# Alternate accumulators from two PSUM pools in the dense stages, and one projection moved into the end of each memory attention

## The chip, the cores and the metric

The kernel runs on one core of one Trainium2 chip. The metric is device microseconds of one execution (us below). The engines are named as the profile names them: PE (matmuls and transposes), DVE and ACT (vector and scalar work, which also read the matmul results), POOL (elementwise work in SBUF only, as this kernel uses it), and SP, whose queue issues most DMAs. Each engine works through its own instructions in the order in which they were written; semaphores make one wait for another.

## The reference, cut to what matters

Two blocks follow one another on 1024 tokens of width 1024, all in float32. The first has two layers. Each layer projects its input, mixes it in a main branch (layer 0: multi-scale causal pooling; layer 1: forgetting attention) and, beside that, in a cross-attention into 256 memory tokens, and ends in a projection, a residual sum and a layer norm. The second block has a gated MLP and an RWKV-7 mixer side by side and then a mixture of 32 experts. For the change only this much must be seen:

```python
def mixer_sublayer(x, mem, w_in, w_mem_kv, w_out, main_fn):
    h = x @ w_in                       # columns [main | mem q | main gate | mem gate]
    u_main = h[..., :D_MAIN]
    q_mem = h[..., D_MAIN:D_MIX]
    g_main = h[..., D_MIX:D_MIX + D_MAIN]
    g_mem = h[..., D_MIX + D_MAIN:]
    y_main = main_fn(u_main)
    y_mem = memory_attention(q_mem, mem, w_mem_kv)
    y = jnp.concatenate([y_main * jax.nn.silu(g_main), y_mem * jax.nn.silu(g_mem)], axis=-1)
    return y @ w_out
...
# layer 0: main_fn = causal_multiscale_pool(u): trailing means over 2, 4, 8, 16 tokens, one linear map per group
# layer 1: main_fn = forgetting_attention(q, k, v, cum); k, v and the forget gates f from x @ w_kv_shared
# block 2: z = h @ w_in2; gMLP on zu, zv; RWKV-7 on zr (decay, inverse of a triangular matrix per chunk, scan)
```

## The kernel before

**Precision and matmuls.** Every operand of a large product is cut into a high and a low part (`split`, L167; for weights `split_one`, L117): ACT casts the high part (`wh`, `xh`), DVE or POOL subtracts it to get the low part (`wl`, `xl`). One product is three matmuls (`mm3`, L161; lines L163 to L165). A *half* of a dense projection (`proj`, L239) is 8 x 3 = 24 matmuls of 512 columns into one PSUM accumulator; `evac` then reads that accumulator on ACT and DVE.

**PSUM.** Two pools of tiles hold the accumulators: `ps1` with two tiles of one bank (`bank`, L173; they appear in the trace as `mm`), and `ps2` with three tiles of two banks (`banks2`, L179; `at`). A pool hands out its tiles in turn. A tile that is handed out again makes the first matmul into it wait until all that read it before are done. Dense stages take `bank()` only; attention logits, transposes and a few sums take `banks2()`.

**Order.** The program is a list of items, executed in order while it is recorded. `weave` (L182) puts *side* functions among *dense* items: after dense item d stand the side functions whose place is at most d (at most `per` of them), and what is left over follows at the end. Weights are loaded and split two uses ahead.

**Memory attention** (`mem_attention`, L325) has 16 dense halves (q and gate of four heads) and eight units (head, half of the tokens). A unit goes through three steps, each one side function later than the last: `logits` (PE into an `at` tile, then DVE maximum, ACT exponentials, DVE scaling into `P`), `turn` (eight transposes of `P` into an `at` tile, ACT and DVE split them into `PTh`, `PTl`) and `values` (six matmuls, then `y_out`). The last unit's `turn` and the last two `values` follow when the dense halves have run out. In layer 1 the first two halves (`self.first`) stand earlier, and the memory's keys and values come back from DRAM by one DMA (`kvt<-kvd`, L735) at `begin_kv`; the first `logits` stands behind the first half that follows.

**Pooling stage of layer 0** (`u_evac` L629, `mix` L667): for each group of 256 channels two projections u (whose evacuation is a chain of shifted sums on DVE, longer for the wider windows), two gates g, then `mix`, two accumulators for each half of the tokens. `mix(g, 0)` stands ahead of the first half of the next group's u, and `mix(g, 1)` behind it. Each accumulator of `mix` is read by `y_out` (L417): one DVE product into `y32`, a tile with a single buffer (L418), which ACT and POOL then split into `yh` and `yl`.

**Layer 1's projections** (`layer1_proj`): the forget gates f (one projection of 16 columns, `w_f`), q and k (16 projections), v (four groups of eight accumulators of 256 columns, split into `vst`, three buffers, each stored to DRAM), gates. Side functions among them form the 48 partial sums of another product on DVE from DMA'd weights (`ad`), and `mod_sum` closes every fourth with a matmul into an `at` tile (L860).

**gMLP projections** (`gmlp_proj`) of block 2 run while DVE still inverts the RWKV triangles step by step (`rwkv_inverse`, L1466 and L1467); its result goes to DRAM (`Tmd`, `Tnd`) and comes back as `N` and `T` for `rwkv_merge` (L1584), which stands among the gMLP's dense items.

Of the kernel before, what the change touches and what calls it, by code (L numbers as in the profile page):

```python
# [45 lines left out]
class Prog:  # L46


    def __init__(self, tc, ins, out):
        self.tc = tc  # L50
        self.nc = tc.nc
        self.i = ins
        self.out = out
        self.items = []
        self.later = []
        self.lst = {}
        self.lag = 2
        self.item = 0
        self.open = {}


# [110 lines left out]

    def bank(self):  # L173
        return self.ps1.tile([128, 512], F32, name="mm", tag="mm")

# [63 lines left out]
    def proj(self, spec, evac, M=128):  # L239
# [13 lines left out]

        return [(first, [spec]), (lambda: half(1), [])]


# [325 lines left out]
    def layer0(self):  # L582
# [22 lines left out]

        self.add(begin_mem)
        d, s = self.mem_attention(0)
        self.weave(d, s)

        def begin_r():  # L610
# [10 lines left out]
            for t in range(16):  # L621
                nc.vector.memset(self.cnt[:, t:t + 1], 1.0 / (t + 1))

        self.add(begin_r)
        ymem = lambda: self.ymem
        U, PM, SG = {}, {}, {}
        self.ymain = {}
# [55 lines left out]
        def ug(g):  # L683
            it = []
            for j in range(2):
                it += self.proj((self.i["w_in"][0, 2 * g + j], 1024, "g"), u_evac(g, j))
            for j in range(2):
# [13 lines left out]

        def end_pool():
            self.close("pg")
            self.lnp = self.pool("ln", right=True)
# [17 lines left out]
    def layer1_proj(self):  # L722
# [11 lines left out]
        def begin_kv():  # L734
            nc.sync.dma_start(self.open_kv(True).bitcast(F32), self.kvd)  # L735
            self.mp = self.pool("mp", right=True)

        self.add(begin_kv)
        self.weave(self.rest, [(k - 2, f) for k, f in self.side])

        def begin():
            self.close("mp", "kv", "mq")
            self.st = self.pool("st", right=True)

        self.add(begin)
# [65 lines left out]

        dense = self.proj((self.i["w_f"], KD * 16, "g"), f_evac, M=16)
        for p in range(8):
# [66 lines left out]
        self.weave(dense, side, 2)  # L880
        self.add(lambda: self.close("st", "xt"))

# [600 lines left out]
    def gmlp_proj(self):  # L1483
        nc = self.nc

        def begin():
            self.close("rw")
            self.gp = self.pool("gp", right=True)
            self.gate1 = self.row(self.gp, self.modd[:, 2 * D:3 * D], "gate")
            gm = self.gm = self.pool("gm", right=True)  # L1490
            self.gv = gm.tile([128, NT, 512], F32, name="gv")
# [116 lines left out]
    def rwkv_chain(self):  # L1608
# [6 lines left out]

        def begin():
            self.close("ps2")
            self.ps2 = self.pool("ps2", 2, PSUM)
# [1152 lines left out]
```

## Time and profile before

| what | value |
|---|---|
| runs shown (3) | 2796.18, 2798.14, 2799.12 us; median 2798.14 |
| profiled execution | 2806.17 us, of which the span of the core's instructions is 2804.4 us |
| busy in the profiled span | PE 2618.7 us (93%), DVE 1759.6 (63%), ACT 1212.4 (43%), POOL 826.8 (29%) |
| mean granted clock of TensorE | 0.966 of 2.4 GHz |
| layer 0, memory attention | from about 60 us to 183 us of the span |
| layer 0, pooling and output | 183 us to 560 us |
| layer 1, memory attention | 565 us to 681 us |
| layer 1, projections | 681 us to 1065 us |
| block 2, gMLP projections | 1729 us to about 1800 us |

The profiled execution took 8.0 us more than the median of the three timed runs. Times of stretches below count from the start of the span. Idle time of PE costs time only where PE is what the rest waits for; a granted clock of 0.5 means that matmuls come half as fast (1.2 GHz in place of 2.4).

### The profile page before, as it was taken

To read this page: it belongs to the slowest core of one execution; us is meant where nothing else is said; L and a number is where in the kernel's file an instruction comes from. 1 tells how busy PE (TensorE), PEld (TensorE's weight loads), DVE (VectorE), ACT (ScalarE), POOL (GpSimd) and SP (SyncE) were. 2 spreads that over 40 slices of the span, in tenths; PEclk is the share of its full clock that TensorE was granted. 3 is DMA by queue.
4 is the path that set the end of the run, shared out by engine and by line. 5 is a ranking of instruction groups with operands and counts; after the bars stand their busy time and mean duration, and the time that the engine had idled before them with its cause. 6 is when DMAs were issued, how large, how long until landed. Compare 5 with 4: busy or idle time off the path is not lost. (4 is left out here: it accounts for less than half of the span.)

```text
span 2804.4 us, 40099 instructions
## 1 busy us (share of the span) xinstructions
PE 2618.7 (93%) x14955; PEld 2131.7 (76%) x14955; DVE 1759.6 (63%) x2560; ACT 1212.4 (43%) x1851; POOL 826.8 (29%) x480
## 2 busy tenths in 40 slices
PE   8999999999999997999986989999995999999996
PEld 7878787776878886888865667987784777777774
DVE  5332334633556314777867769633657998899998
ACT  5331212333212213667643522323433767677773
POOL 1122323612222121112145432323362332233324
PEclk9999999999999998999998999999996999999999
DMA  7121111311787537655522465466327999899995
GB/s 267 33 91 49 42 48 43 112 55 38 257 299 263 192 104 219 167 156 168 137 79 73 134 188 180 97 156 151 99 95 263 355 349 344 303 376 368 368 367 206
DMA packets 284886, 511.43 MB, mean 182 GB/s; under 512 B 122651, under 2 KB 166027, under 8 KB 284432
## 3 DMA queue, kind: packets, MB, share of 16 engines
q1 hardware_dynamic: 275040, 491.26, 53.5%
q0 software_dynamic: 9360, 16.52, 1.6%
q8 instruction: 119, 1.95, 0.3%
q10 hardware_dynamic: 288, 1.05, 0.1%
q14 instruction: 79, 0.65, 0.1%
HBM read 437.53 MB, written 97.18 MB: 191 GB/s over the span
## 5 line engine op out<-in xcount | busy, mean ns | idle before, releaser
L128 POOL TENSOR_TENSOR wl<-raw,wh 128x1024 fp32r<-128x1024 f32 (+2 forms) x111 | 281.1, 2541 | 663.4 <-ACT wh L126 653.7
L171 DVE TENSOR_TENSOR wl<-raw,wh 128x1024 fp32r<-128x1024 f32 x384 | 452.0, 1223 | 37.8 <-ACT wh L169 37.7
L163 PE MATMUL mm<-xh,wh 128*128 128x512 f32 (+3 forms) x1136 | 452.6, 398 | 12.9 <-DVE y L419 8.5
L165 PE MATMUL mm<-xh,wl 128*128 128x512 f32 (+3 forms) x1136 | 450.4, 397 | 0.7 <-POOL wl L128 0.7
L164 PE MATMUL mm<-xl,wh 128*128 128x512 f32 (+3 forms) x1136 | 450.1, 396 | 0.8 <-DVE xl L171 0.8
L169 ACT CAST wh<-raw 128x1024 fp32r<-128x1024 f32 x384 | 382.7, 1049 | 54.3 <-PE mm L165 21.4
L163 PEld LDWEIGHTS mm<-xh,wh 128*128 128x128 f32 (+3 forms) x1136 | 213.4, 188 | 73.7 <-issue 11.5
L164 PEld LDWEIGHTS mm<-xl,wh 128*128 128x128 f32 (+3 forms) x1136 | 213.4, 188 | 53.2 <-issue 2.0
L165 PEld LDWEIGHTS mm<-xh,wl 128*128 128x128 f32 (+3 forms) x1136 | 213.4, 188 | 50.3 <-POOL wl L128 1.1
L163 PE MATMUL mm<-wh,xth 128*128 128x512 f32 x496 | 202.1, 408 | 2.1 <-ACT xth L169 1.1
L164 PE MATMUL mm<-wl,xth 128*128 128x512 f32 x496 | 200.2, 404 | 3.2 <-DVE wl L171 2.9
L165 PE MATMUL mm<-wh,xtl 128*128 128x512 f32 x496 | 196.7, 397 | 0.0
L126 ACT CAST wh<-raw 128x1024 fp32r<-128x1024 f32 (+1 forms) x139 | 140.0, 1023 | 75.8 <-PE mm L165 74.4
L2408 POOL DMA_INDIRECT ymd<-yo,si x32 | 53.0, 1657 | 381.0 <-DVE yo L2451 377.3
L163 PE MATMUL mm<-wh,yh 128*128 128x512 f32 x384 | 160.2, 417 | 1.5 <-DVE y L419 1.1
L410 DVE SCALAR_TENSOR_TENSOR sg<-sg,mm 128x512 f32<-128x512 f32 x48 | 33.0, 688 | 196.0 <-ACT sg L409 196.0
L163 PE MATMUL mm<-wh,xh 128*128 128x256 f32 x512 | 147.0, 287 | 9.0 <-DVE vst L171 4.0
L164 PE MATMUL mm<-wl,yh 128*128 128x512 f32 x384 | 153.5, 400 | 1.7 <-POOL wl L128 1.7
L165 PE MATMUL mm<-wh,yl 128*128 128x512 f32 x384 | 152.9, 398 | 0.0
L164 PE MATMUL mm<-wl,xh 128*128 128x256 f32 x512 | 143.5, 280 | 0.0
L165 PE MATMUL mm<-wh,xl 128*128 128x256 f32 x512 | 143.4, 280 | 0.0
L2403 POOL DMA_INDIRECT xg<-h2d,gi x33 | 117.2, 3550 | 57.7 <-PE at L2414 27.9
(546 smaller groups left out, 5777.3 us busy)
## 6 DMA issues: line engine op xcount, KB each, us to landing
raw<-in_w_moe_dram SPq DMA_DIRECT2D x382, 512.0 KB
raw<-in_w_in_dram SPq DMA_DIRECT2D x48, 512.0 KB
ad<-in_ada_w_dram SPq DMA_DIRECT2D x48, 512.0 KB
raw<-in_w_out_dram SPq DMA_DIRECT2D x32, 512.0 KB
ymd<-zd SPq DMA_DIRECT2D x16, 512.0 KB
vd<-vst SPq DMA_DIRECT2D x32, 256.0 KB
qa<-qd SPq DMA_DIRECT2D x32, 256.0 KB
kb<-kd SPq DMA_DIRECT2D x32, 256.0 KB
```

Of the source, the lines that this page charges most:

```text
L126: self.nc.scalar.copy(h[:p], r[:p])
L128: e.tensor_tensor(l[:p], r[:p], h[:p].bitcast(F32), ALU.subtract)
L163: mm(ps, ah, bh, start=start, stop=False)
L164: mm(ps, ah, bl, start=False, stop=False)
L165: mm(ps, al, bh, start=False, stop=stop)
L169: self.nc.scalar.copy(h, src)
L171: e.tensor_tensor(l, src, h.bitcast(F32), ALU.subtract)
L410: nc.vector.scalar_tensor_tensor(sg, sg, 1.0, ps, op0=ALU.add, op1=ALU.mult)
L2403: self.nc.gpsimd.indirect_dma_start(out=xg, out_offset=None, in_=self.h2d[:, :], in_offset=bass.IndirectOffsetOnAxis(ap=gi, axis=0), bound ...
L2408: self.nc.gpsimd.indirect_dma_start(out=self.ymd[:, :], out_offset=bass.IndirectOffsetOnAxis(ap=si, axis=0), in_=y, in_offset=None, bounds ...
```

## The change

Three things change. A flag `wide` makes `bank()` hand out tiles of the two pools in turn: one time the first half of a two-bank `at` tile, the next time an `mm` tile. The flag is on in the pooling stage of layer 0 (from `begin_r` to `end_pool`), in layer 1's projections (from `begin` to `end`) and from the start of the gMLP projections to the start of the RWKV chain. Second, `proj_held` is a projection whose two halves write the two halves of one `at` tile, and whose evacuation is a list of items of its own; with it the next stage's first projection (layer 0: the first u; layer 1: f) is appended to the dense halves of the memory attention, and its evacuation stands where the projection stood. Third, in layer 1's memory attention no side function stands ahead of the second dense half.

```diff
@@ def bank(self)
+        if self.wide:
+            self.turnabout = not self.turnabout
+            if self.turnabout:
+                return self.banks2()[:, 0:512]
         return self.ps1.tile([128, 512], F32, name="mm", tag="mm")
...
+    def proj_held(self, spec, evac, M=128):
+        hold = {}
+        def half(h):
+            wh, wl = hold["w"]
+            ps = hold["ps"][:M, h * 512:h * 512 + 512]
+            for k in range(KD):
+                self.mm3(ps, wh[:, k], wl[:, k], self.xh[h][:, k], self.xl[h][:, k], k == 0, k == KD - 1)
+        def first(w):
+            hold["w"] = [t.rearrange("p (k n) -> p k n", k=KD) for t in w]
+            hold["ps"] = self.banks2()
+            half(0)
+        out = [(lambda h=h: evac(h, hold["ps"][:M, h * 512:h * 512 + 512]), []) for h in range(2)]
+        return [(first, [spec]), (lambda: half(1), [])], out
...
@@ def layer0(self)
         d, s = self.mem_attention(0)
-        self.weave(d, s)
+        held, u00 = self.proj_held((self.i["w_in"][0, 0], 1024, "g"), u0)
+        self.weave(d + held, s)
...
+            self.wide = True
...
-                it += self.proj((self.i["w_in"][0, 2 * g + j], 1024, "g"), u_evac(g, j))
+                it += u00 if g + j == 0 else self.proj((self.i["w_in"][0, 2 * g + j], 1024, "g"), u_evac(g, j))
...
         def end_pool():
+            self.wide = False
...
@@ def layer1_proj(self)
+        held, fs = self.proj_held((self.i["w_f"], KD * 16, "g"), lambda h, ps: f_evac(h, ps), M=16)
         self.add(begin_kv)
-        self.weave(self.rest, [(k - 2, f) for k, f in self.side])
+        self.weave(self.rest + held, [(max(k - 2, 1), f) for k, f in self.side])
...
+            self.wide = True
...
-        dense = self.proj((self.i["w_f"], KD * 16, "g"), f_evac, M=16)
+        dense = list(fs)
...
+        def end():
+            self.wide = False
+            self.close("st", "xt")
```

**Place 1, PE at the end of layer 0's memory attention.** Of each block of matmuls the first row stands here: before, the third-last unit's `values` (`mm_1481`), then the last `turn` (`at_1492`), the last two `values`, and the two halves of the first u (`mm_1580`, `mm_1620`) and of the second.

```order
L163 MATMUL mm_1481<-PTh_1363,kvt_119 128x512
...
L367 MATMUL at_1492<-ident_75,P_1458 128x128 x8
L163 MATMUL mm_1505<-PTh_1477,kvt_119 128x512
...
L163 MATMUL mm_1518<-PTh_1501,kvt_119 128x512
...
L163 MATMUL mm_1580<-xh0_112,wh_1264 128x512
...
L163 MATMUL mm_1620<-xh1_113,wh_1264 128x512
...
L163 MATMUL mm_1662<-xh0_112,wh_1380 128x512
```

The same place in the changed kernel:

```order
L164 MATMUL mm_1481<-PTh_1363,kvt_119 128x512
...
L164 MATMUL at_1498<-xh0_112,wh_1264 128x512
...
L391 MATMUL at_1523<-ident_75,P_1458 128x128 x8
L164 MATMUL mm_1536<-PTh_1477,kvt_119 128x512
...
L164 MATMUL at_1498<-xh1_113,wh_1264 128x512
...
L164 MATMUL mm_1573<-PTh_1532,kvt_119 128x512
...
L164 MATMUL at_1661<-xh0_112,wh_1380 128x512
```

The two halves of the first u (24 matmuls each) now stand one ahead of the last `turn` and one ahead of the last `values`, both in the tile `at_1498`; the second u begins in another `at` tile. At the end of layer 1's memory attention the halves of f stand in the same two places.

**Place 2, DVE in the pooling stage,** around the first u half of the group with window 16, between `mix(2, 0)` and `mix(2, 1)`; `y` is the product of `y_out`, `sw` and `pm` are the chain of sums. Before:

```order
L419 SCALAR_TENSOR_TENSOR y_3082<-mm,psc,sg 128x512
L636 MEMSET u 128x16
L642 COPY carry<-u 128x16
L648 TENSOR_TENSOR sw<-u 128x527
L648 TENSOR_TENSOR sw<-sw 128x525
L648 TENSOR_TENSOR sw<-sw 128x521
L648 TENSOR_TENSOR sw<-sw 128x513
L651 SCALAR_TENSOR_TENSOR pm<-sw,u 128x512
...
L654 TENSOR_TENSOR pm<-sw,u 128x15
L419 SCALAR_TENSOR_TENSOR y_3145<-mm,psc,sg 128x512
L419 SCALAR_TENSOR_TENSOR y_3156<-mm,psc,sg 128x512
```

In the changed kernel:

```order
L443 SCALAR_TENSOR_TENSOR y_3081<-mm,psc,sg 128x512
L666 MEMSET u 128x16
L672 COPY carry<-u 128x16
L678 TENSOR_TENSOR sw<-u 128x527
L678 TENSOR_TENSOR sw<-sw 128x525
L678 TENSOR_TENSOR sw<-sw 128x521
L678 TENSOR_TENSOR sw<-sw 128x513
L681 SCALAR_TENSOR_TENSOR pm<-sw,u 128x512
...
L684 TENSOR_TENSOR pm<-sw,u 128x15
L443 SCALAR_TENSOR_TENSOR y_3144<-mm,psc,sg 128x512
L443 SCALAR_TENSOR_TENSOR y_3155<-at,psc,sg 128x512
```

No DVE instruction moves; the second accumulator of `mix(2, 1)` now lies in an `at` tile.

**Place 3, PE at the start of layer 1's memory attention.** First rows of the blocks before: the first half after `begin_kv`, the first `logits` (`at_4025`), the next half, the second `logits`, the first `turn`.

```order
L163 MATMUL mm_3996<-xh1_3479,wh_3831 128x512
...
L163 MATMUL at_4025<-kvt_3991,qh_3925 128x256
...
L163 MATMUL mm_4051<-xh1_3479,wh_3835 128x512
...
L163 MATMUL at_4079<-kvt_3991,qh_4021 128x256
...
L367 MATMUL at_4105<-ident_75,P_4041 128x128 x8
```

In the changed kernel:

```order
L164 MATMUL mm_3995<-xh1_3478,wh_3830 128x512
...
L164 MATMUL mm_4024<-xh1_3478,wh_3834 128x512
...
L164 MATMUL at_4052<-kvt_3990,qh_3924 128x256
...
L164 MATMUL mm_4084<-xh0_3477,wh_3893 128x512
...
L164 MATMUL at_4113<-kvt_3990,qh_4020 128x256
```

The first `logits`, the first reader of the DMA'd `kvt`, stands one dense half later.

## Rows read from the trace of the kernel before

**Rows 1.** The page: busy time, share of the span and count of PE, and PE's clock.

```profile
PE 2618.7 (93%) x14955; PEld 2131.7 (76%) x14955; DVE 1759.6 (63%) x2560; ACT 1212.4 (43%) x1851; POOL 826.8 (29%) x480
PEclk9999999999999998999998999999996999999999
```

**Rows 2.** Timeline of PE, one middle unit: start, duration, instruction, [idle before, releaser].

```profile
94.57 0.28 PE L163 MATMUL at<-kvt,qh 128*128 128x256 f32 x1
...
96.01 1.04 PE L367 MATMUL at<-ident,P 128*128 128x128 f32 x8
96.81 0.48 PE L163 MATMUL mm<-PTh,kvt 128*128 128x512 f32 x1
...
98.28 0.39 PE L163 MATMUL mm<-xh,wh 128*128 128x512 f32 x1
```

**Rows 3.** Timeline of PE, end of layer 0's memory attention.

```profile
167.97 0.28 PE L163 MATMUL at<-kvt,qh 128*128 128x256 f32 x1
...
173.80 1.46 PE L367 MATMUL at<-ident,P 128*128 128x128 f32 x8 [1.97 <-DVE P L359]
...
182.73 0.63 PE L163 MATMUL mm<-xh,wh 128*128 128x512 f32 x1
```

**Rows 4.** Timeline of PE, end of layer 1's memory attention.

```profile
666.25 0.28 PE L163 MATMUL at<-kvt,qh 128*128 128x256 f32 x1
...
680.97 0.63 PE L163 MATMUL mm<-xh,wh 128*16 128x512 f32 x1
```

**Rows 5.** Windows: length, busy of PE PEld DVE ACT POOL, PE's clock, DMA share, GB/s.

```profile
182.73:186.02 3.29, 3.29 (x9) 2.61 (x8) 0.69 (x1) 1.56 (x2) 1.81 (x3) 0.50 0.62 167
338.98:346.00 7.02, 7.02 (x24) 5.60 (x25) 0.83 (x2) 1.22 (x2) 3.81 (x3) 0.76 0.00 0
439.92:448.00 8.08, 8.08 (x24) 6.47 (x25) 0.83 (x2) 1.21 (x2) 3.79 (x3) 0.66 0.00 0
570.41:577.00 6.59, 6.59 (x25) 5.85 (x26) 1.49 (x3) 1.94 (x8) 0.00 (x0) 0.64 0.00 0
1732.00:1750.00 18.00, 13.10 (x90) 12.70 (x89) 17.70 (x16) 5.75 (x8) 7.16 (x2) 0.81 0.59 183
1789.10:1797.00 7.90, 7.90 (x159) 7.69 (x160) 6.87 (x11) 2.54 (x5) 5.96 (x5) 0.78 0.67 179
1073.66:1084.00 10.34, 7.93 (x24) 6.30 (x25) 3.56 (x11) 3.53 (x9) 0.00 (x0) 0.51 1.07 360
1720.00:1771.00 51.00, 45.48 (x330) 42.83 (x330) 50.36 (x39) 14.52 (x23) 21.29 (x7) 0.93 0.40 127
```

**Rows 6.** Timeline of PE, three waits in the pooling stage.

```profile
285.78 0.51 PE L163 MATMUL mm<-xh,wh 128*128 128x512 f32 x1 [1.59 <-DVE y L419]
...
338.98 0.51 PE L163 MATMUL mm<-xh,wh 128*128 128x512 f32 x1 [3.11 <-DVE y L419]
...
439.92 0.79 PE L163 MATMUL mm<-xh,wh 128*128 128x512 f32 x1 [3.85 <-DVE y L419]
```

**Rows 7.** Timeline of DVE, ahead of the third of these waits.

```profile
433.95 1.29 DVE L642 COPY carry<-u 128x16 f32<-128x16 f32 x1 [3.12 <-ACT u L639]
...
439.12 0.74 DVE L419 SCALAR_TENSOR_TENSOR y<-mm,psc,sg 128x512 f32<-128x512 f32 x1
```

**Rows 8.** Timeline of DVE, end of the pooling stage.

```profile
492.12 0.75 DVE L419 SCALAR_TENSOR_TENSOR y<-mm,psc,sg 128x512 f32<-128x512 f32 x1 [2.05 <-POOL yl L171]
```

**Rows 9.** Timeline of PE, start of layer 1's memory attention.

```profile
570.41 0.55 PE L163 MATMUL at<-kvt,qh 128*128 128x256 f32 x1 [4.70 <-DMA kvt<-kvd]
```

**Rows 10.** Waits of PE and of ACT, 720 to 1062 us: total, times, longest.

```profile
PE mm L163 <- DVE vst L171: 4.0, 6, 1.6
...
ACT vst L169 <- DMA vd<-vst: 49.8, 17, 5.7
```

**Rows 11.** Timeline of PE: the wait for `N`, and the first matmul of layer 1's attention.

```profile
1789.10 1.07 PE L1584 MATMUL mm<-N,L 32*32 32x32 f32 x57 [2.00 <-DMA N<-Tnd]
...
1073.66 0.45 PE L940 MATMUL at<-kb,qa 128*128 128x128 f32 x1 [9.12 <-DMA kb<-kd]
```

More of the change, by code (lines that the diff above doesn't have):

```diff
@@ L59, in __init__ @@
         self.open = {}
+        self.wide = self.turnabout = False
     def pool(self, name, bufs=1, space=None, right=False):
@@ L606, in layer0, with u0 @@
         self.add(begin_mem)
+        U, PM, SG = {}, {}, {}
+        def u0(h, ps):
+            u_evac(0, 0)(h, ps)
         d, s = self.mem_attention(0)
-        self.weave(d, s)
+        held, u00 = self.proj_held((self.i["w_in"][0, 0], 1024, "g"), u0)
+        self.weave(d + held, s)
         def begin_r():
@@ L622, in begin_r @@
                 nc.vector.memset(self.cnt[:, t:t + 1], 1.0 / (t + 1))
+            self.wide = True
         self.add(begin_r)
         ymem = lambda: self.ymem
-        U, PM, SG = {}, {}, {}
         self.ymain = {}
@@ L880, in layer1_proj @@
         self.weave(dense, side, 2)
-        self.add(lambda: self.close("st", "xt"))
+        def end():
+            self.wide = False
+            self.close("st", "xt")
+        self.add(end)
     def layer1_fox(self):
@@ L1489, in begin @@
             self.gate1 = self.row(self.gp, self.modd[:, 2 * D:3 * D], "gate")
+            self.wide = True
             gm = self.gm = self.pool("gm", right=True)
@@ L1616, in begin @@
         def begin():
+            self.wide = False
             self.close("ps2")
```

## The prediction, written before the changed kernel was run

> **What bounds the kernel now.** The page comes first: PE is busy for 93% of the span and no other engine for more than 76%, and its clock stands at full speed in most of the 40 slices [rows 1]. So time is to be had only where PE stands still or runs at half clock, and the change can touch three such kinds of place. I read the list of PE's waits, then the timeline of PE around each wait in the stages that the change touches, and last the windows, which give the clock behind each wait. The reader is to see four things. At the end of each memory attention PE has nothing left but a chain of short steps that wait for the softmax [rows 3, 4]. In the pooling stage PE waits three times for `y`, the read of an accumulator, and the row shows a plain projection (`mm<-xh,wh`) waiting: its operands are there, the bank is not [rows 6]. At the start of layer 1's attention PE waits for a DMA [rows 9]. And behind each of these waits the granted clock is at 0.5 for some microseconds [rows 5], so that a wait costs more than its own length. A clock c over a window of w us costs w x (1 - c).
>
> **The change, part by part.** No matmul, evacuation or DMA is added or removed; the sum consists of waits that go or come.
>
> A. *End of layer 0's attention.* From the last `logits` to the first matmul of the next stage the trace takes 182.73 - 167.97 = 14.76 us [rows 3]. The work in it is one `logits`, two `turn` and three `values`. A middle unit shows what these take without waits: 96.01 - 94.57 = 1.44, 96.81 - 96.01 = 0.80, 98.28 - 96.81 = 1.47 [rows 2]; together 1.44 + 1.60 + 4.41 = 7.45. So 7.3 us are lost there, and the next 3.29 us run at 0.50, which loses 1.65 [rows 5]: 8.95 in all. In the changed order a half of 24 matmuls stands between the last `logits` and the last `turn`, and one ahead of the last `values`. Per half that is 24 x 0.229 = 5.5 us (a `values` has six such matmuls in 1.47 to 0.23 each). The wait for `P` to be covered is 1.97 [rows 3]. Both halves cover with margin, so I take all 8.95. What these halves covered before also counts: behind the attention they ran while pools closed and loads landed. Now the second u does that. It has a free `at` tile and a free `mm` tile for its first two halves, some 11 us; only the third half needs an `at` tile that could still be held. I cost this at nothing.
>
> B. *Pooling stage.* The waits of 1.59, 3.11 and 3.85 [rows 6] come from two accumulators in turn: `y` of `mix(g, 1)` stands on DVE behind the whole chain of sums of the u half just evacuated (433.95 to 439.12 in the widest group [rows 7]), and PE's next half needs that `y`'s bank. With tiles taken from both pools in turn, the next half gets a tile whose reader was done a half earlier, so the wait goes, and DVE has until the next `mix`, some six halves on, to catch up. Behind the second and third wait the clock costs 7.02 x 0.24 = 1.7 and 8.08 x 0.34 = 2.7 [rows 5]. Sum: 8.55 + 4.4 = 12.95, which I take as 13.0. Two further waits for `y` stand at the end of the stage, and these I do not count: there four `y` follow one another through the single `y32` buffer, the last at 492.12 [rows 8], `wide` is off for the output items behind it, and the second of those needs just the bank that the last `y` reads. With or without the earlier waits PE gets past it at about 492.9.
>
> C. *Start of layer 1's attention.* The wait for `kvt` is 4.70 [rows 9] and the clock behind it costs 6.59 x 0.36 = 2.4 [rows 5]: 7.1. The half put ahead takes 5.5 > 4.70, so the wait goes, with 0.8 us to spare. Bounds: 6.1 (the DMA a little later) to 7.1.
>
> D. *End of layer 1's attention.* The same pattern: 680.97 - 666.25 = 14.72 [rows 4], less 7.45 is 7.3, and a stretch at half clock as long as A's: 9.0.
>
> E. *v projections.* PE waits for the read of `vst` in six places, 4.0 us [rows 10]. Behind them stands ACT, which waits for the store of an earlier `vst` (49.8 us in 17 waits). More accumulators let PE run two quanta further ahead, which hides a late store but doesn't make stores faster. Bounds 0 and 4.0; I take 3.0, since the longest single wait (1.6) is shorter than one quantum of 24 x 0.12 = 2.9 us (0.12 is a `logits` matmul of the same 256 columns: 1.44 / 12 [rows 2]).
>
> F. *gMLP projections.* Here too two accumulators run short: PE is idle for 18.00 - 13.10 = 4.9 us and the clock is at 0.81 [rows 5], together some 7 to 8 us. But DVE is busy for 50.36 of 51.00 us in this stretch [rows 5]; it works through the inverse, and PE meets the inverse's result soon after, where it already waits 2.0 us for `N` [rows 11]. If PE comes 7.7 us earlier, it waits 9.7 there. Worse, one long wait in place of several short ones can cost more clock: now 7.90 x 0.22 = 1.7 [rows 5]; behind the wait of 9.12 [rows 11] it is 10.34 x 0.49 = 5.1 [rows 5]. Bounds: -3.4 (all of that difference) to +8 (if `N` came as much earlier as PE does). DVE's share speaks for the low end; the loads behind the inverse may go out a little earlier, as POOL frees earlier. I take -2.0.
>
> Sum: 8.95 + 13.0 + 7.1 + 9.0 + 3.0 - 2.0 = 39.05. The profiled execution took 2806.17, so it would take 2767.1; it lies 8.0 above the median, and I subtract from the median: 2798.14 - 39.05 = **2759.1**.
>
> **The rivals.**
> *More accumulators only move the wait* (B and E give nothing, as F). For it: DVE, ACT and the stores work no faster, and in the pooling stage a chain of sums takes about as long as a half. Against: DVE is free for most of that stage, as the gates behind u have no chain of sums, so the backlog has time to drain. Left are A + C + D + F = 23.05: 2775.1.
> [...]
>
> *The cover is missed elsewhere.* The held tile is one of three; it comes free only when its evacuation is done, and that stands behind the closing of pools, a constant's DMA and a bias DMA. If PE's third half has to wait for it, A and D each give back about what they gained: 2759.1 + 18 = 2777. Against: 11 us of other halves stand in between.
>
> *F gains after all:* `N` follows PE. At the upper bound the sum is 10 larger: 2749. Against: DVE's 50.36 of 51.00.
>
> *Slower than before:* in layer 1's projections `mod_sum` now draws its `at` tile from the same ring as the projections, and PE stands behind DVE's partial sums there. There are 12 of them; to eat 39 us each must wait 3.3 us. Before, the list of PE's waits in that stretch has no line but the one for `vst`, 4.0 in all [rows 10], so none of the 12 waited as it was. Some wait here is possible, 3.3 each is not likely: 2800.
>
> *The change does nothing:* the rows of the changed order show the tiles alternating and the halves moved, so only a loss that happens to equal the gain leaves the time where it was.
>
> **How the numbers follow.** Chances: forecast 0.66; accumulators only move the wait 0.12; cover missed 0.08; F gains 0.09; slower 0.03; no change 0.02. The likeliest gives 2759. Its own spread, from the bounds of C, E and F's low end and about 5 us for B, is 2752 to 2768. To leave out no more than 2 in 10 the range takes in the two rivals of 2775 and 2777 and nearly all of 2749: 2748 to 2778. A difference of 0.2% (5.6 us) is about what a measurement of this kernel can tell from none. All cases but the last two are faster by more than that: faster 0.95, same 0.02, slower 0.03.
>
> **What would show each step right or wrong.** A and D: no wait for `P` or `PTh` at either end of attention, the first matmul of the held projection directly behind the third-last `values`, and full clock there. B: no wait of a projection for `y`, but the two at the end of the stage still there, with the last `y` of the stage as far behind its first `mix` as before. C: no wait for `kvt`, or one below 1 us. E: the waits for `vst` below 1 us in all. F: no wait for `gv` or `z` at the gMLP's start, and a wait for `N` of about 10 us with a longer stretch at half clock behind it. What would make the prediction wrong: PE waiting for u's or f's evacuation some 11 us behind the attention, waits at L860's matmuls, or a wait for `N` as short as before.

## The result, and the profile after

| | changed kernel | kernel before |
|---|---|---|
| median | 2763.19 us (2760.01 to 2763.59, 4 runs) | 2798.63 us (2796.18 to 2800.24, 4 runs) |
| ratio | 0.9856, 95% interval 0.9838 to 0.9874 | |
| span, mean granted clock in the profile | 2758.2 us, 0.977 | 2804.4 us, 0.966 |

The medians are 35.4 us apart, where 39 were forecast. The ratio and its interval are the ones on record; they are not the quotient of the two medians (0.9873), and a ratio of 0.9856 would be 40 us. So the total is known to some 5 us, and the terms have to be read from the traces. The page of the changed kernel, PE's busy time and clock (compare [rows 1]):

```profile
PE 2594.9 (94%) x14955; PEld 2118.6 (77%) x14955; DVE 1772.4 (64%) x2560; ACT 1210.8 (44%) x1851; POOL 819.8 (30%) x480
PEclk9999999999999999999998999999997999999999
```

The windows of the changed kernel that answer to [rows 5]: the end of layer 0's attention, the pooling stage without its end, the start and the end of layer 1's attention, layer 1's projections, the gMLP up to `N`, and the wait for `N`:

```profile
165.00:180.00 15.00, 15.00 (x81) 12.81 (x80) 5.13 (x10) 5.43 (x13) 4.00 (x3) 1.00 0.12 36
...
190.00:450.00 260.00, 260.00 (x1128) 211.19 (x1127) 103.85 (x175) 56.70 (x83) 86.41 (x50) 1.00 0.16 51
...
540.00:565.00 25.00, 25.00 (x136) 21.45 (x135) 11.97 (x20) 8.07 (x22) 2.43 (x1) 1.00 0.26 97
640.00:660.00 20.00, 20.00 (x92) 12.08 (x91) 5.56 (x10) 7.99 (x15) 7.92 (x5) 1.00 0.09 28
680.00:1018.00 338.00, 338.00 (x1827) 282.35 (x1826) 154.14 (x189) 66.30 (x105) 75.18 (x30) 1.00 0.66 227
1684.00:1736.00 52.00, 52.00 (x435) 51.66 (x434) 49.92 (x48) 15.12 (x26) 19.35 (x9) 1.00 0.51 128
1736.00:1746.00 10.00, 3.63 (x75) 3.29 (x74) 8.47 (x16) 0.94 (x2) 4.58 (x4) 0.77 0.64 134
```

In the first six PE is busy for all of the time and the clock is at 2.4 GHz throughout; the seventh is what is left. The timeline of PE at the end of layer 0's attention, against [rows 3]: the last `logits`, the held first half of u, the last `turn`, the held second half, and the second u. No row has a wait.

```profile
167.88 0.28 PE L164 MATMUL at<-kvt,qh 128*128 128x256 f32 x1
...
171.57 0.39 PE L164 MATMUL at<-xh,wh 128*128 128x512 f32 x1
...
177.06 1.03 PE L391 MATMUL at<-ident,P 128*128 128x128 f32 x8
...
179.32 0.39 PE L164 MATMUL at<-xh,wh 128*128 128x512 f32 x1
...
186.19 0.39 PE L164 MATMUL at<-xh,wh 128*128 128x512 f32 x1
```

Of the waits in the stages read here, those at the end of the pooling stage stay (the second is the `y` of [rows 8]), and those for `N` and for `kb` [rows 11]. Timeline of PE of the changed kernel:

```profile
464.02 0.50 PE L164 MATMUL mm<-wh,yh 128*128 128x512 f32 x1 [0.66 <-DVE y L443]
...
469.61 0.50 PE L164 MATMUL mm<-wh,yh 128*128 128x512 f32 x1 [2.53 <-DVE y L443]
...
1029.53 0.44 PE L977 MATMUL at<-kb,qa 128*128 128x128 f32 x1 [9.15 <-DMA kb<-kd]
...
1741.83 0.28 PE L1622 MATMUL at<-N,L 32*32 32x32 f32 x2 [4.95 <-DMA N<-Tnd]
1743.53 0.69 PE L1622 MATMUL at<-N,L 32*32 32x32 f32 x18 [1.42 <-DMA N<-Tnd]
```

**Where the time came from.** The same matmul can be looked up in two traces. Its start in the first trace of before less its start in another one is that kernel's *lead* there; at the first `kb` matmul it is 1073.66 - 1029.53 = 44.13. Between two points the lead grows by what the stage gained. Below is the middle value of nine matmuls in a row, for the kernels of the experiments too (us; the left column is the time in before's first trace).

| at | after | before, 2nd trace | after, 2nd trace | wide only | held only | held, early psc | one half | mix alone |
|---|---|---|---|---|---|---|---|---|
| 160, l0 attention | 0.1 | 0.0 | -0.2 | -0.2 | 0.3 | 0.0 | 0.2 | 0.2 |
| 200, behind it | 9.1 | 2.0 | 8.8 | 1.1 | 9.2 | 9.0 | 5.2 | 9.1 |
| 260 | 9.1 | 2.0 | 8.8 | 0.6 | 0.7 | 9.0 | 5.2 | 9.1 |
| 460 | 23.3 | 2.6 | 23.0 | 14.9 | 1.8 | 10.8 | 19.5 | 20.6 |
| 510, behind pooling | 23.3 | 2.6 | 23.0 | 14.9 | 1.8 | 10.9 | 19.5 | 14.3 |
| 590, in l1 attention | 30.2 | 5.1 | 28.3 | 15.9 | 8.7 | 16.2 | 26.4 | 21.2 |
| 700, behind it | 39.0 | 5.9 | 37.1 | 16.8 | 17.5 | 24.3 | 32.9 | 29.3 |
| 1060, behind l1 proj. | 44.2 | 5.9 | 37.1 | 18.7 | 17.1 | 25.9 | 33.5 | 31.0 |
| 1725, ahead of gMLP | 43.5 | 2.3 | 33.8 | 16.0 | 15.3 | 23.5 | 28.7 | 30.1 |
| 1830, behind `N` | 45.1 | -0.2 | 34.1 | 16.8 | 16.7 | 25.2 | 29.3 | 30.6 |
| 2700 | 46.2 | -0.7 | 34.4 | 17.0 | 18.8 | 27.9 | 31.9 | 30.8 |

The terms of the prediction against two pairs of traces, each the step of the lead between the two lines that enclose the stage (for the second pair, the third column less the second):

| term | forecast | first pair | second pair |
|---|---|---|---|
| A, end of l0 attention | 8.95 | 9.0 | 7.0 |
| B, pooling stage | 13.0 | 14.2 | 13.6 |
| C, wait for `kvt` | 7.1 | 6.9 | 2.8 |
| D, end of l1 attention | 9.0 | 8.8 | 8.0 |
| E, v projections | 3.0 | 5.2 | 0.0 |
| F, gMLP | -2.0 | 1.6 | 2.8 |
| stages the change does not touch | 0 | 0.4 | 1.0 |
| sum | 39.05 | 46.1 | 35.2 |

One trace gives a stage no better than to some microseconds: from 1060 to 1725 us, where no kernel here differs from before, the steps of the lead run from -4.8 to 0.5 us over the thirteen traces.

### The profile page after: what moved, and what is told of

It reads as the page before. It is cut to its first block, busy times and chain, and to the rows that moved or that the text cites. A ratio compares the mean times of both kernels' runs of the same rounds, so it can differ in the third digit from the quotient of the medians.

```text
span 2758.2 us, 40093 instructions
## 1 busy us (share of the span) xinstructions
PE 2594.9 (94%) x14955; PEld 2118.6 (77%) x14955; DVE 1772.4 (64%) x2560; ACT 1210.8 (44%) x1851; POOL 819.8 (30%) x480
## 5 line engine op out<-in xcount | busy, mean ns | idle before, releaser
L164 PE MATMUL mm<-xh,wh 128*128 128x512 f32 (+2 forms) x792 | 316.2, 399 | 3.7 <-DVE ca L1301 2.6
L165 PE MATMUL mm<-xl,wh 128*128 128x512 f32 (+2 forms) x792 | 312.6, 395 | 0.8 <-DVE xl L172 0.8
L166 PE MATMUL mm<-xh,wl 128*128 128x512 f32 (+2 forms) x792 | 312.2, 394 | 0.7 <-POOL wl L129 0.7
L164 PEld LDWEIGHTS mm<-xh,wh 128*128 128x128 f32 (+2 forms) x792 | 148.7, 188 | 44.4 <-issue 5.4
L165 PEld LDWEIGHTS mm<-xl,wh 128*128 128x128 f32 (+2 forms) x792 | 148.7, 188 | 35.9 <-issue 1.8
L166 PEld LDWEIGHTS mm<-xh,wl 128*128 128x128 f32 (+2 forms) x792 | 148.4, 187 | 35.5 <-POOL wl L129 1.1
L166 PE MATMUL at<-xh,wl 128*128 128x512 f32 (+1 forms) x344 | 135.3, 393 | 0.0
L164 PE MATMUL at<-xh,wh 128*128 128x512 f32 (+1 forms) x344 | 135.2, 393 | 0.0
L165 PE MATMUL at<-xl,wh 128*128 128x512 f32 (+1 forms) x344 | 134.9, 392 | 0.0
L2442 POOL DMA_INDIRECT xg<-h2d,gi x33 | 114.9, 3481 | 57.7 <-PE at L2453 27.9
L999 ACT ACTIVATE pp<-pp,fst 128x128 f32<-128x128 f32 (+7 forms) x128 | 99.9, 781 | 63.1 <-DVE fst L992 61.7
```

What stands on the lines that cost most here:

```text
L164: mm(ps, ah, bh, start=start, stop=False)
L165: mm(ps, ah, bl, start=False, stop=False)
L166: mm(ps, al, bh, start=False, stop=stop)
L999: nc.scalar.activation(p[:, :n], p[:, :n], AF.Exp, bias=st[:, i:i + 1], scale=-1.0, accum_out=st[:, 8 + i:9 + i])
L2442: self.nc.gpsimd.indirect_dma_start(out=xg, out_offset=None, in_=self.h2d[:, :], in_offset=bass.IndirectOffsetOnAxis(ap=gi, axis=0), bound ...
```

## The experiments

Times are medians; with each stands the ratio on record to runs of the kernel before on the same chip (its median there was 2802.21, 2805.01 and 2801.89 us for the first four, the next four and the last four kernels).

**1. The kernel before once more.** No edit.

> The kernel before once more, for a second profile of it. The first profiled execution took 2806.2 us, 8 us above the median of its timed runs, and the changed kernel's first profile gains 46 us on it where the timed medians differ by 35. Theory: the 8 us are chance of that one execution (which half-clock stretches fall where), so this profile comes out near 2798 and the difference lies in stages that the change does not touch. Rival: a profiled execution of this kernel is always some 8 us longer, then it comes out near 2806 again.

Measured: 2806.41 us (10 runs, 2794.77 to 2812.01), ratio 1.0006 [0.9992, 1.0021]; the profiled execution took 2808.89, its span 2807.2. Neither theory is held up as it was put: this execution was long as well, yet timed runs of the same program spread from 2794 to 2812. What the second trace does show is that the stages are not as long each time. Windows around the end of layer 0's attention and behind the wait for `kvt`, and that wait in PE's timeline:

```profile
165.00:190.00 25.00, 20.98 (x94) 16.33 (x93) 8.71 (x33) 7.84 (x16) 7.09 (x5) 0.93 0.61 207
567.00:574.00 7.00, 6.54 (x34) 5.68 (x35) 2.57 (x7) 1.94 (x8) 0.00 (x0) 1.00 0.00 0
...
567.46 0.36 PE L163 MATMUL at<-kvt,qh 128*128 128x256 f32 x1 [2.71 <-DMA kvt<-kvd]
```

The same first window in the first trace of before:

```profile
165.00:190.00 25.00, 21.27 (x86) 16.10 (x84) 7.65 (x13) 7.28 (x16) 7.10 (x5) 0.80 0.56 195
```

In the attention's end the waits are nearly the same (for `P` 4.0 us in two, one at each attention, as in the first trace) and the clock is higher, 0.93 against 0.80; so A loses 2 us less in this execution than in the one that the sum was made from. The wait for `kvt` is 2.71 in place of 4.70, and no half clock follows it, where [rows 5] has 0.64. But here a stretch at half clock lies ahead of the wait (0.51 over 558.90 to 562.30; the first trace has full clock in that half), so that by the lead C loses 2.5 us less, and not the 4 that the wait and the clock behind it would give.

**2. Only the alternating accumulators.** The two held projections and the later first `logits` are taken back:

```diff
...
-        self.weave(d + held, s)
+        self.weave(d, s)
...
-                it += u00 if g + j == 0 else self.proj((self.i["w_in"][0, 2 * g + j], 1024, "g"), u_evac(g, j))
+                it += self.proj((self.i["w_in"][0, 2 * g + j], 1024, "g"), u_evac(g, j))
...
-        self.weave(self.rest + held, [(max(k - 2, 1), f) for k, f in self.side])
+        self.weave(self.rest, [(k - 2, f) for k, f in self.side])
...
-        dense = list(fs)
+        dense = self.proj((self.i["w_f"], KD * 16, "g"), f_evac, M=16)
```

> Only the alternating accumulators, no held projection, layer 1's side functions where they were. Theory (the stages' gains are local and add up): the two ends of attention and the DMA wait stand as before, 9 + 7 + 9 = 25 us are lost again, the pooling stage gains 14, the v projections 6 and the gMLP 1.5: 2798.6 - 21.5, about 2777. Rival (accumulators only move waits): near 2798, with new waits of PE later in the same stages.

Measured: 2787.84 us, ratio 0.9945 [0.9927, 0.9963]: between the theory's 2777 and the rival's 2798. PE's waits from 160 to 700 us (total, times, longest) have those of the two attentions again, and of `y` only the end of the stage:

```profile
PE at L164 <- DMA kvt<-kvd: 4.4, 1, 4.4
PE at L391 <- DVE P L383: 3.9, 2, 2.0
PE mm L164 <- DVE y L443: 3.2, 2, 2.5
PE mm L164 <- ACT PTh L170: 2.3, 2, 1.2
```

The lead grows by 14.3 from 260 to 460 us, so the pooling stage's gain needs no held projection. What the theory had too high is the rest: in the gMLP the lead grows by 0.8 (1725 to 1830), not by 1.5, and in the v projections by 1.9 (700 to 1060), not by 6: the waits for `vst` are gone, and in their place stands another (total, times, longest; 700 to 1040 us):

```profile
PE at L891 <- DVE acc L883: 3.4, 4, 1.2
```

That is `mod_sum`, the place of the slower rival, but what is late is not its accumulator: it is the partial sum `acc` itself. PE comes there sooner, and DVE itself waits there for the DMA of its weights `ad` (2.3 us in four).

**3. Only the held projections.** `self.wide = True` is taken out in all three places.

> Only the held projections and the later first logits; bank() hands out mm tiles alone everywhere. Theory: A 9.0 + C 6.9 + D 8.8 = 24.7 us of the gain stay: about 2774. Rival (the held halves only pay because the wide stage behind them absorbs the late evacuation): PE waits for u's or f's accumulator behind the attention, and the time is above 2780.

Measured: 2789.58 us, ratio 0.9958 [0.9942, 0.9974]: the rival. The lead is 9.2 at 200 us and 0.7 at 260. The timelines of PE, DVE and ACT there:

```profile
203.04 0.79 PE L164 MATMUL mm<-xh,wh 128*128 128x512 f32 x1 [5.86 <-ACT u L668]
...
195.29 0.17 DVE L649 TENSOR_SCALAR psc<-psc 128x8 f32<-128x8 f32 x1 [8.30 <-DMA psc<-in_pool_scale_dram]
...
198.12 0.58 ACT L668 COPY u<-at 128x512 f32<-128x512 f32 x1
...
202.41 0.58 ACT L668 COPY u<-mm 128x512 f32<-128x512 f32 x1
```

PE has filled the second u's two `mm` tiles and wants one of them back; ACT reads it at 202.41 only, since it takes the u halves in order with DVE's chain of sums between them, and DVE began with the first at 195.3, when the DMA of `psc` had landed. Behind the wait the clock falls as well (0.62 over 203.04 to 210.00). At the end of layer 1's attention nothing of that kind follows (8.8 us gained from 590 to 700): f is read by one ACT instruction a half.

**4. The flag off in the gMLP alone.** `self.wide = True` is taken out of `gmlp_proj`.

> The changed kernel with the flag left off in the gMLP projections. My prediction had the flag cost 2 us there (a longer wait for N): then this kernel is 2 us faster, about 2761. By the changed kernel's trace it gains 1.5 us (PE enters the stage 43.5 us ahead of before and leaves the wait for N 45.1 us ahead): then about 2764.5. The times can hardly tell 3 us; the trace does: the lead over before just behind the wait for N is 43.5 by the second, 47 by the first.

Measured: 2762.87 us, ratio 0.9863 [0.9846, 0.9881], the changed kernel's time, between the two forecasts of 2761 and 2764.5. PE's waits from 1680 to 1760 us:

```profile
PE mm L164 <- ACT gv L1534: 3.3, 1, 3.3
PE mm L1621 <- DMA N<-Tnd: 1.5, 1, 1.5
PE mm L164 <- DVE z L1298: 1.4, 1, 1.4
```

The lead goes from 41.6 at 1725 us to 45.2 at 1830, and with the flag from 43.5 to 45.1. Behind the wait the lead is between the 43.5 and 47 that were expected, and both kernels have the same. That fits `N` setting the end, with the flag only choosing where PE waits; experiments 9 and 10 test it.

**5. Held only, with the two constants early** (`psc` and `cnt` built at the start of the attention, in place of behind the loads of `r`):

```diff
         def begin_mem():
+            self.psc = self.const.tile([128, 8], F32, name="psc")
+            nc.sync.dma_start(self.psc, self.i["pool_scale"])
...
         def begin_r():
-            self.psc = self.pg.tile([128, 8], F32, name="psc")
-            nc.sync.dma_start(self.psc, self.i["pool_scale"])
...
-            self.wide = True
```

> The held-only kernel (bank() hands out mm tiles alone), with one thing more: the two small constants of the pooling stage, psc and cnt, are loaded and built at the start of the memory attention, in place of behind the eight loads of r. The held-only kernel won 9.2 us at the end of layer 0's attention and gave 8.6 back 20 us later: PE waited 5.86 us for ACT's read of u, ACT stood behind DVE, and DVE had waited 8.30 us for the DMA of psc. Theory: with the constants there, DVE starts on u's halves at once, the wait of 5.86 goes, and the lead over before at 260 us is 9 in place of 0.7; the run is 8 us shorter than held-only, about 2781. Rival: two mm tiles are too few for three u halves in a row whatever DVE does, then 3 us or more of the wait stay.

Measured: 2782.22 us, ratio 0.9925 [0.9895, 0.9955]. The wait of 5.86 is gone, and the lead is 9.0 at 260 us. The window over the attention's end and the u halves:

```profile
165.00:260.00 95.00, 95.00 (x427) 77.74 (x426) 31.52 (x50) 20.37 (x34) 26.54 (x15) 1.00 0.27 92
```

So it was the constants' place, and by DVE's row above the DMA of `psc` (the edit moves the building of `cnt` too). In the changed kernel DVE waits for it too (8.25 us), and the spare `at` tile covers that.

**6. One half held, the other behind the attention,** in both layers:

```diff
-        self.weave(d + held, s)
+        self.weave(d + held[:1], s)
+        self.add(*held[1][:1])
...
-        self.weave(self.rest + held, [(max(k - 2, 1), f) for k, f in self.side])
+        self.weave(self.rest + held[:1], [(max(k - 2, 1), f) for k, f in self.side])
+        self.add(held[1][0])
```

> The changed kernel with one half of the held projection put among the attention's last steps (ahead of the last turn) and the other behind the attention, in both layers. Theory: the wait for P goes, the two waits for PTh and PTl (1.16 and 0.46 idle, 2.6 us with the restart of PE) stay in each layer, and as a wait ends in a stretch at half clock each time, some 1.7 more: the lead at 200 us is 9.0 - 4.3 = 4.7, and the run is 5 to 9 us longer than the changed kernel, about 2770. Rival: the wait for P is what lowers the clock; then the clock stays full and 2.6 are lost in each: about 2768, lead at 200 us 6.4.

Measured: 2770.26 us, ratio 0.9874 [0.9848, 0.9899]. In both layers the wait for `P` is gone and the two others stay, with the same numbers. Windows over the two ends, and PE's waits at the first:

```profile
178.00:188.00 10.00, 8.09 (x28) 5.93 (x28) 2.51 (x3) 2.25 (x3) 4.90 (x3) 0.83 0.67 231
651.00:661.00 10.00, 8.09 (x34) 3.82 (x33) 2.51 (x3) 2.26 (x4) 4.01 (x3) 1.00 0.19 55
...
PE mm L164 <- ACT PTh L170: 1.2, 1, 1.2
PE mm L165 <- DVE PTl L172: 0.8, 1, 0.8
```

In layer 0 half clock followed, and the lead behind it is 5.2, nearer to the theory's 4.7 than to the rival's 6.4; in layer 1 it did not, and the stage gains 6.5 in place of 8.8 (590 to 700), a loss of 2.3, near the rival's 2.6. Each half pays for its own waits; whether the clock falls on top is not decided by them.

**7. The store of `Tnd` first.** In the changed kernel SP's queue has 15 us between its first store of the inverse's result and its load of `N`:

```profile
1724.78 0.38 SPq L1510 DMA_DIRECT2D Tmd<-z  x1
1725.21 7.00 SPq L1513 DMA_DIRECT2D Tmd<-TT  x2
1732.31 3.86 SPq L1515 DMA_DIRECT2D Tnd<-LT  x1
1736.22 0.43 SPq L1602 DMA_DIRECT2D wCd<-wC  x1
...
1739.62 0.48 SPq L1614 DMA_DIRECT2D N<-Tnd  x1
```

```diff
-            for b in range(2):
-                s = slice(32 * b, 32 * b + 32)
-                nc.sync.dma_start(Tm[:, s, s], w["T"][:, b])
             V.tensor_copy(w["L"][:, 0].rearrange("p t c -> p t c"), w["T"][:, 0].rearrange("p c t -> p t c"))
             nc.sync.dma_start(self.Tnd.rearrange("p e c s t -> (p e c) s t"), w["L"][:, 0])
+            for b, e in ((1, nc.sync), (0, nc.scalar)):
+                s = slice(32 * b, 32 * b + 32)
+                e.dma_start(Tm[:, s, s], w["T"][:, b])
```

> The changed kernel with the stores at the end of the inverse in another order: the store of Tnd, for which the load of N waits, first on SP, then one block of Tmd, and the other block of Tmd on ACT's queue. In the changed kernel SP spent 3.38, 3.53 and 3.86 us on the three stores, Tnd's last. Theory: N comes some 5 us earlier, the wait of 4.95 for it shrinks below 1 us and with it the half clock behind it; 5 to 8 us faster than the changed kernel, about 2757. Rival: ACT's issue of 3.4 us holds up the reads of gv and PE waits there instead, or a load other than N's is what sets the end: no gain, 2763.

Measured: 2762.14 us, ratio 0.9844 [0.9818, 0.9870]: the rival's time, no gain that can be told. SP's queue in it:

```profile
1729.57 0.38 SPq L1510 DMA_DIRECT2D Tmd<-z  x1
1732.68 3.36 SPq L1512 DMA_DIRECT2D Tnd<-LT  x1
1736.10 0.43 SPq L1515 DMA_DIRECT2D Tmd<-TT  x1
1736.58 4.78 SPq L1602 DMA_DIRECT2D wCd<-wC  x1
...
1741.88 0.49 SPq L1614 DMA_DIRECT2D N<-Tnd  x1
```

The load of `N` goes out 12.3 us behind `Tmd<-z` in place of 14.8, half of the 5 us that the theory wanted, and PE still waits 6.4 us for `N` in two waits, the longer of 4.6. Read together, the two queues show why. In both, the long rows are those right behind a store into `Tmd` (3.38, 3.53 and 3.86 in the first, the first two merged above; 3.36 and 4.78 in the second), and the row behind the store of `Tnd` is short (0.43 in each). So it seems to be the stores into `Tmd` that hold the queue, each in the row behind it, and not the store of `Tnd`, whose own row is long where it follows one. The edit moved the cheap store ahead and left a block of `Tmd` between it and the load of `N`. The load of `N` ahead of all blocks of `Tmd` was not tried. By the lead this kernel gains 2.5 us from 1725 to 1830, where the changed kernel's two traces gain 1.6 and 0.3. Of the rival's reasons, the wait for `gv` isn't there.

**8. Only `mix`'s accumulators from the `at` tiles** in the pooling stage (flag off there, constants early as in 5):

```diff
-                ps = self.bank()
+                ps = self.banks2()[:, 0:512]
```

> The changed kernel with the flag off in the pooling stage; there only the accumulators of mix (the ones that y reads) are taken from the at tiles, all projections from the mm tiles; the constants psc and cnt are early, as in the kernel above, so that u's evacuation isn't late. Theory (the waits of the pooling stage were for y's accumulators alone): no wait of a projection there, the lead over before at 460 us is 23 as in the changed kernel, and the time is that of the changed kernel, about 2763. Rival (each dense half needs the spare accumulators): some 13 us of waits for u or y come back, about 2776.

Measured: 2776.08 us, ratio 0.9899 [0.9870, 0.9927]: my theory falls. The time is the rival's, the way there is not: of its some 13 us of waits for `u` or `y` there are 1.8. PE's waits from 190 to 500 us:

```profile
PE mm L165 <- POOL wl L129: 2.2, 1, 2.2
PE mm L164 <- ACT wh L127: 1.9, 1, 1.9
PE mm L164 <- ACT u L668: 1.8, 2, 1.2
PE mm L164 <- DVE sg L434: 1.8, 1, 1.8
PE mm L164 <- DVE r L485: 1.2, 1, 1.2
```

No projection waits for `y`. But with that wait gone the next readers in DVE's and ACT's queues are late for the two `mm` tiles (`u`, `sg`, `r`), and at the end of the stage PE meets weights that are not yet split. From 260 to 460 us the lead grows by 11.5 in place of 14.2, and 6.3 are lost at the end, where the clock is at 0.90 too (455 to 485 us). Behind the stage this kernel is 9.0 us behind the changed one's first trace (14.3 against 23.3); what it loses further on lies in stages that the edit does not touch. The profile's list names the wait that comes first; what is needed is a spare tile for whichever reader is late.

**9 and 10. The merge two items later, with the flag and without it in the gMLP:**

```diff
-        d += 8
+        d += 10
```

> The changed kernel with the first matmuls of the merge, which wait for N, two v/u quanta later among the gMLP's items (some 5.7 us of PE's work). Theory: N sets the end of the gMLP stage in the changed kernel (PE waited 4.95 and 1.42 us there), so what the flag wins at the stage's start is given back at N; with the merge later the waits shrink below 1.5 us and the run is 5 to 8 us shorter than the changed kernel, about 2757; the lead over before behind the merge is 48 to 50 us in place of 45. Rival: behind the merge something else is late as well (the chain's loads of the merged result), then the lead falls back to 45 within the next 40 us.

> The same with the flag off in the gMLP projections. Theory: the waits for gv's reads (1.36 and 3.30 us) stand again and N is no longer waited for, so this kernel is 5 us longer than the one with the flag, about 2762, and hardly shorter than with the merge in its old place. Rival (the flag gives nothing in this stage): as long as the one above.

Measured: 2755.69 us, ratio 0.9836 [0.9816, 0.9856], with the flag; 2759.40, ratio 0.9846 [0.9830, 0.9861], without. PE's waits from 1680 to 1800 us, with the flag:

```profile
PE at L1622 <- DMA N<-Tnd: 0.7, 1, 0.7
```

and without:

```profile
PE mm L164 <- ACT gv L1534: 3.4, 1, 3.4
PE mm L164 <- DVE z L1298: 1.4, 1, 1.4
```

From 1725 to 1830 us the lead grows by 9.1 with the flag (40.7 to 49.8, as the theory had it) and by 5.1 without (39.6 to 44.8), and both keep it to the end (52.2 and 47.4 at 2700), so the rival falls. The kernel of experiment 11, with the flag and the late merge, gains 7.0 there. So the flag is worth 2 to 4 us in the gMLP as soon as `N` is hardly waited for: 7.0 or 9.1 less 5.1 by the leads, 3.7 by the medians, whose runs spread over 10 us with the flag.

**11 and 12. Three waits removed, and the changed kernel once more:**

```diff
-        d += 8
+        d += 10
...
-                side.append((6 + m, mod_sum))
+                side.append((9 + m, mod_sum))
...
-        t = pool.tile([128, 512], F32, name="y32", tag="y32", bufs=1)
+        t = pool.tile([128, 512], F32, name="y32", tag=tag, bufs=1)
...
-                self.y_out(self.pg, y, h, ps, self.psc[:, c:c + 1], SG.pop((g, j, h)))
+                self.y_out(self.pg, y, h, ps, self.psc[:, c:c + 1], SG.pop((g, j, h)), "pm" if g == 3 and j else "y32")
```

> Three small changes on top of the changed kernel, each against a wait that its runs left: the merge two quanta later; mod_sum three items later (in five of six runs with the flag PE waited 1.0 to 3.4 us there for acc, in place of vst); and in the last group of the pooling stage every second y of mix in pm's buffer, which is free there, so that four y no longer follow one another through one y32 (waits of 0.66 and 2.53, and 1.76 for wl behind them). Theory: 6 + 2 + 3 = 11 us shorter than the changed kernel, about 2752. Rival for the third: POOL's work on yl and wl sets the end there and the wait moves to wl, then 1 us or less of it is won.

> The changed kernel once more, beside the one above on the same chip. Theory: near 2763; its trace shows one to four waits of mod_sum for acc, as five of six kernels with the flag did and its first trace did not, so that its gain over before in the v projections is 2 to 4 us and not 6.

Measured: 2748.83 us, ratio 0.9810 [0.9795, 0.9825], and 2765.37 us, ratio 0.9864 [0.9849, 0.9880]: 16.5 us between them on one chip, where 11 were forecast. By the leads the end of the pooling stage gains 4.3 (23.4 at 460, 27.7 at 510, where the changed kernel gains nothing, so the rival falls), the v projections 4.9 (41.8 to 46.7), the gMLP 7.0 (44.8 to 51.8). Of the waits at the pooling stage's end only this is left, and in layer 1's projections none:

```profile
PE mm L165 <- POOL wl L129: 1.1, 2, 0.7
```

The changed kernel's second trace, from 700 to 1025 us, has the wait that its first one had not, and its gain in the v projections is 0.0, below the 2 to 4 expected:

```profile
PE at L893 <- DVE acc L885: 2.3, 2, 1.6
```

## Why the prediction was right, point by point

**The sum.** 39 forecast, 35.4 and 36.5 measured by the medians (2798.63 - 2763.19; 2801.89 - 2765.37). The sum was made from one execution and taken off a median. Of its terms 10.1 us were clock (1.65 in each of A and D, 4.4 in B, 2.4 in C), and the second trace of before shows that such a term is not the same each time. The waits for `y`, `P` and `PTh` came back to within 0.1 us, the one for `kvt` did not. That the total came within 4 us is in part luck: against the second pair of traces A, C, D and E together are 10 us less than forecast, and B, F and the stages that the change does not touch 6 us more. Three readings were loose without moving the sum much. Behind the first wait of the pooling stage the clock is full (1.00 over 285.78 to 292.00), so not every wait was followed by half clock. Within A's 7.3 us the clock is already down (0.61 over 173.80 to 182.73), so more of A was clock than the 1.65. And six matmuls in 1.47 us make 0.245 each, not 0.23; the held half has 24 in 177.06 - 171.57 = 5.49 us, which is the 0.229 that the sum used.

**A and D** held: 9.0 and 8.8 of 8.95 and 9.0; the waits for `P`, `PTh` and `PTl` are gone. That what the halves covered before "costs nothing" was right for the kernel as it is, for the reason given (a free `at` and a free `mm` tile), and experiment 3 prices the cover: 8.6 us. The rival "the cover is missed elsewhere" is real in mechanism, with the constant's DMA that it named; the flag in the next stage keeps it away. The two parts of the change are thus not independent: alone they gain 14.4 and 12.6 us, together (without the flag in the gMLP) 39.3, by 2802.21 less 2787.84, 2789.58 and 2762.87. Of the 12 us between, experiment 3 explains 8.6; by the leads most of the rest lies in stages that the change does not touch.

**B** held in size (14.2 and 13.6 of 13.0). One step was too narrow: I put the gain down to `y`'s accumulators alone, and experiment 8 shows that spare tiles for the projections are needed as well. The two waits at the stage's end stayed, as forecast.

**C** held against the first trace (6.9 of 7.1), and was 2.8 against the second. Of the difference 2.5 us are the second trace of before, and 1.6 the changed kernel's second trace, which runs at a lower clock shortly ahead of the attention (0.89 over 530 to 545 us, 1.00 in its first trace). The bounds of 6.1 to 7.1 were too tight: the DMA itself comes 2 us sooner in one execution than in another (2.71 and 4.70), which I had only let come later.

**E** is the term that was wrong in its working. "PE's waits for `vst` below 1 us" came true, and so did a part of the slower rival: PE waits 1.0 to 3.4 us for `acc` in `mod_sum` instead, in eight of the nine traces with the flag there and the sums in their old place. The step that failed is "more accumulators let PE run two quanta further ahead, which hides a late store": they do, and PE then meets DVE's sums too soon. DVE's own waits for the DMA of `ad` go with it: 1.0 to 2.3 us in those eight traces, 0.6 in the one where PE does not wait. E is 5.2 or 0.0 by the pair of traces; against before's first trace all nine give 0.0 to 5.2 with 2.0 in the middle, and the two kernels without the flag in that stage (experiments 3 and 5) -0.4 and 1.6. So E is nearer 2 than the 3.0 forecast, and hardly clear of the scatter. Its upper bound was too low as well: with `mod_sum` later and no wait at all the stage gains 4.9, where the listed idle was 4.0 [rows 10]; the matmul behind a wait is longer too (0.51 in [rows 6], 0.39 in [rows 2]), which may be the rest.

**F** was right in its mechanism. The waits for `gv` and `z` go, the wait for `N` grows from 2.0 [rows 11] to 6.4 in all and to 8.7 in the second trace; 9.7 was forecast. The longer stretch at half clock came too: behind the wait the clock is 0.68 over 1741.83 to 1752.00 (0.59 over 1752 to 1762 in the second trace), which by the prediction's formula is 3.3 and 4.1 us where before lost 1.7; 5.1 was forecast. From 1725 to 1830 us the lead grows by 1.6 and 0.3 in the changed kernel's two traces and by 3.6 with the flag off there alone (experiment 4), but by 1.4 and 1.6 in the two other kernels without it (experiments 3 and 5), so a cost of the flag there, 0 to 3 us by the leads, is not clear of the scatter; the medians can't tell it either. Against before, for which the -2.0 was given, the stage gained 1.6 and 2.8: its first matmul with `N` came 1 to 2 us sooner after the start of the stage than in the first trace of before, and more against the second. So the size and the sign of F were wrong, and why `N` comes sooner was not tried.

**Where spare accumulators gave nothing.** The Trainium skill's page "TensorE: Matmul & The Clock Gate", section "HAM oscillation — how this bites in real kernels", says of a matmul kernel whose loop had been reordered to keep PE at full clock: "Adding PSUM double-buffering gave no further gain (125.5 µs)." It doesn't say what that kernel still waited for. Here the gMLP stage is such a place as long as PE waits there for `N`, which comes by DMA: the ratios to before are 0.9863 without the spare accumulators and 0.9856 and 0.9864 with them. The pooling stage is not: there DVE and ACT are the late ones, and the lead grows by 14.

## What to carry to other kernels

A spare accumulator pays where the reader that is late has time to catch up before the next wait of PE, and pays nothing where what follows is fixed by something else: look for the next operation that PE cannot have sooner (here `N` and `acc`), and move that first; then the same spare accumulators were worth 2 to 4 us more in the gMLP; for `acc` the gain was measured together with two other edits. Work moved to cover a wait leaves the place that it covered before: look there for the slowest small thing, such as a constant's DMA behind eight large loads. And take the clock's share of a wait from more than one execution before it goes into a sum.

## What the runs showed of the hardware that was not expected

With one half held, two ends of attention have the same waits (1.2 and 0.8 us), the same PE busy time (8.09 of 10.00 us) and different granted clocks, 0.83 and 1.00: waits of this size do not lower the clock each time. The kernel before, run again, spreads over 2794 to 2812 us.

On SP's queue the row that takes long is the one behind a store of 512 KB into `Tmd`, which is written in blocks of 32 x 32: 3.4 to 3.9 us in the changed kernel, 3.36 and 4.78 in experiment 7, and 9.77 for the first two such rows together in the second trace of before. The store's own row can be short (0.38 for `Tmd<-z`). Behind the store of `Tnd`, which holds as many bytes, the row took 0.43. Everything behind on that queue waits, so what a store costs is to be looked for in the row behind it.
